# Filter norms and skip terms of a long convolution, from rows on every partition to channels on the partitions

## The chip, the cores and the metric

The kernel runs on one core of a Trainium2 chip. The core has a matrix engine (TensorE; PE in the profile, with its weight loads PEld), a vector engine (DVE), a scalar engine (ACT), GpSimd (POOL) and SyncE (SP), whose queue issues most DMAs. Each engine runs its own instructions in the order in which they were recorded and waits on semaphores for the others. The metric is the time of one execution on the device in microseconds (us), as the median of several runs.

## The reference

One layer of an encoder block over 2048 positions of width 1024, in float32. What matters here is the Hyena branch, 512 channels wide: two long convolutions, each with a filter of 4096 taps per channel that a small network generates. The filter is scaled to norm 1 per channel, and each convolution adds its input times a factor `d` per channel (the skip term):

```python
    h = h * decay[:, None, None, :]
    h_fwd = h[:, :, 0]
    h_bwd = h[:, :, 1]
    k = jnp.concatenate([h_fwd[:1] + h_bwd[:1], h_fwd[1:], jnp.zeros_like(h_fwd[:1]),
                         h_bwd[1:][::-1]], axis=0)
    return k * lax.rsqrt(jnp.sum(k * k, axis=0, keepdims=True) + EPS)
...
    uf = jnp.fft.rfft(uf32, n=2 * l, axis=1)
    y = jnp.fft.irfft(uf * k_freq[None], n=2 * l, axis=1)[:, :l]
    return (y + uf32 * d.astype(jnp.float32)).astype(u.dtype)
...
    z = v
    for n, gate in enumerate((x1, x2)):
        z = gate * fft_long_conv(z, k_freq[:, n], long_d[n])
    return z
```

Before this branch come the normed projection, and beside it a 2-D Fourier mix; after it the output projection and an MLP of width 4096.

## The kernel before

The stages follow each other: projection (to about 415 us), Fourier mix and filters side by side (to about 637), the two convolutions ("hyena"), output projection, and the two MLP products. All matrix products that must be exact to float32 are made of three products of a split operand: `split` writes a rounded part (`kh`) and a rest (`kl`).

The filters are computed in `filters`, in eight units: `Unit(ct, n)` is the block of 128 channels `ct` (0 to 3) of convolution `n` (0, 1); units 0 to 3 belong to n = 0, units 4 to 7 to n = 1. Positions lie on the partitions, channels along the free axis. A unit goes through four steps.

- `generate(q)`, q = 0 to 7: four matmuls into `pk`, times the decay on DVE (`kt`), the split into `kh` and `kl` (for units 1 and 4 both parts lie in one tile `k`), the square on ACT (`sqr`, one buffer), and its sum into `acc` on POOL. At q = 7 POOL folds acc to 128x128.
- `normalise`: from the sum over positions come the reciprocal root (the norm of the filter) and the skip term. Tap 0 sits on partition 0; its value `k0` becomes `k0 + d * v * rsqrt(v)`, where v is the sum of squares plus EPS, so that after the later scaling with rsqrt(v) the skip term d is left. The matmul with a matrix of ones gives the same sums on all 128 partitions, and DVE works on 128x128, then on one partition with 128 elements. It writes tap 0 of kh and kl, and a row of `norms`.
- `stage1(c)`, c = 0 to 7: three matmuls (`pk1`) on kh and kl and a transposition on DVE into `Gk`.
- `stage2(q)`, q = 0 to 7: four matmuls (`pk2`) on Gk, a copy on ACT (`ks`), and a DMA of the spectrum to DRAM.

The spectra are not scaled by the norms; `scale` multiplies the convolutions' first input `zz` by the product of both norms instead, half of it on POOL and half on DVE.

Units overlap: while unit i is in stage1 and stage2, unit i + 2 is generated, and unit i + 1 is normalised early in stage2 of unit i (`if i and new and q == 1`). The order that a reader of the code sees is not the order on each engine: the scheduler of the tile framework sets the instructions of an engine by priority and by when its own estimates say that they are ready, and the program keeps that order. A small matmul or a tiny DVE instruction can so come to stand ahead of work that the code names earlier. All PSUM tiles come from one ring of 8 banks (`pa`).

`rsqrt` is a helper: a square root on ACT (`sq_k`), a reciprocal on DVE (`rc_k`) and one Newton step (`nw_k`); tiles of one column take a shorter form with scalars from the tile.

Of the kernel before, what the change touches and what calls it, by code (L numbers as in the profile page):

```python
# [10 lines left out]
F32 = mybir.dt.float32  # L11
# [3 lines left out]
ALU = mybir.AluOpType  # L15

EPS = 1e-5
# [110 lines left out]
P = 128  # L128
# [6 lines left out]
def hybrid_block(ctx: ExitStack, tc: tile.TileContext, A, out):  # L135
    nc = tc.nc
# [24 lines left out]
    def pool(name, side="left"):  # L161
        return tc.tile_pool(name=name, bufs=1, side=side, reuse_waits="tile")

    def pa(nm):
        return ps.tile([P, 512], F32, tag="a", name=nm, bufs=8)

    def load(pl, tag, shape, src, bufs=1):
        t = pl.tile(shape, F32, tag=tag, name=tag, bufs=bufs)
        nc.sync.dma_start(t, src)
        return t  # L170

    ident = load(cpool, "ident", [P, P], A["ident"])
    gmix = load(cpool, "gmix", [P, 8], A["g_mix"])
    ones = cpool.tile([P, P], F32, tag="ones", name="ones")
    nc.vector.memset(ones, 1.0)

    def split(hi, lo, src, scale=None, eng=None):

        if scale is None:
            nc.scalar.copy(hi, src)  # L180
            (eng or nc.vector).tensor_sub(lo, src, hi)  # L181
        else:
            nc.scalar.mul(hi, src, scale)  # L183
            nc.vector.scalar_tensor_tensor(out=lo, in0=src, scalar=scale, in1=hi, op0=ALU.mult, op1=ALU.subtract)
# [7 lines left out]
    def rsqrt(v, pl, nm, keep=None):  # L192

        s, r = (pl.tile(list(v.shape), F32, tag=f"{a}_{nm}", name=f"{a}_{nm}") for a in ("sq", "rc"))
        q = pl.tile(list(v.shape), F32, tag=f"nw_{nm}{keep or ''}", name=f"nw_{nm}", bufs=keep)
        nc.scalar.sqrt(s, v)
        nc.vector.reciprocal(r, s)
        if v.shape[1] == 1:

            nc.vector.tensor_scalar(out=q, in0=r, scalar1=r, scalar2=v, op0=ALU.mult, op1=ALU.mult)  # L200
            nc.vector.tensor_scalar(out=q, in0=q, scalar1=-0.5, scalar2=1.5, op0=ALU.mult, op1=ALU.add)
            nc.vector.tensor_scalar(out=q, in0=q, scalar1=r, scalar2=None, op0=ALU.mult)
            return q
        nc.vector.tensor_mul(q, r, r)
        nc.vector.tensor_mul(q, q, v)
        nc.vector.tensor_scalar(out=q, in0=q, scalar1=-0.5, scalar2=1.5, op0=ALU.mult, op1=ALU.add)
        nc.vector.tensor_mul(q, r, q)
        return q
# [261 lines left out]
    def filters(ctx, fp, gp, zp, zzs, norms, emb, wo, e1k, f2):  # L470
# [2 lines left out]
        e1h, e1l = (fp.tile([P, P], FR, tag=n, name=n) for n in ("e1h", "e1l"))  # L473
        split(e1h, e1l, e1k)

        class Unit:
            def __init__(self, ct, n):
                self.ct, self.n = ct, n
# [34 lines left out]
                    nc.gpsimd.tensor_add(self.acc[:, 0, :], self.acc[:, 0, :], self.acc[:, 1, :])  # L513

            def normalise(self):
                p = pa("psum_k")
                nc.tensor.matmul(p[:, 0:128], lhsT=ones, rhs=self.acc[:, 0, :], start=True, stop=True)
                v = fp.tile([P, 128], F32, tag="vk", name="vk")
                nc.vector.tensor_scalar(out=v, in0=p[:, 0:128], scalar1=EPS, scalar2=None, op0=ALU.add)
                sc = rsqrt(v, fp, "k")  # L520
                nc.vector.tensor_copy(norms[:, self.n, self.ct], sc)

                dk = fp.tile([1, 128], F32, tag="dk", name="dk")
                nc.sync.dma_start(dk, A["long_d"][:, 2 * self.ct + self.n, :])
                nc.vector.tensor_mul(dk, dk, v[0:1, :])
                nc.vector.tensor_mul(dk, dk, sc[0:1, :])
                nc.vector.tensor_add(dk, dk, self.k0)
                hi, lo = (t[0:1, :, 0, :] for t in self.k)
                k0 = dk.rearrange("p (c j) -> p c j", c=8)
                nc.vector.tensor_copy(hi, k0)  # L530
                nc.vector.tensor_sub(lo, k0, hi)
                if self is units[7]:
                    nc.gpsimd.tensor_mul(norms[:, 0], norms[:, 0], norms[:, 1])

            def scale(self, q, eng):
                z = zzs[0][:, 4 * q : 4 * q + 4, 128 * self.ct : 128 * self.ct + 128]
                eng.tensor_mul(z, z, norms[:, 0, self.ct : self.ct + 1, :].broadcast_to([P, 4, 128]))

            def stage1(self, c):
                if c == 0 and self is units[7]:  # L540
# [18 lines left out]
        units = [Unit(ct, n) for n in range(2) for ct in range(4)]  # L559
# [11 lines left out]
        for i, u in enumerate(units):  # L571
# [12 lines left out]
            for q in range(8):  # L584
# [14 lines left out]
                j = 8 * i + q - 50  # L599
# [690 lines left out]
    with pool("ip") as ip, pool("cp1") as cp1:  # L1290
        with pool("cp0", "right") as cp0:
            run(project(ip, fx, (cp0, cp1), (1, 2), None), filter_hidden(cp0), fourier_weights(cp0))
        zstack, tabs, early = (ctx.enter_context(ExitStack()) for _ in range(3))
# [26 lines left out]

        run(project(ip, fx, (None, cp1), (-1, 0), uf), tables())
        e1f, e1k, turn, gy, e1z, wo, emb, f2 = got
    norms = early.enter_context(pool("norms", "right")).tile([P, 2, 4, 128], F32, tag="norms", name="norms")
    with pool("filters") as fp:
        zzs = []
        gp = early.enter_context(pool("gk", "right"))
        spx = early.enter_context(ExitStack())
        filt = filters(spx, fp, gp, zp, zzs, norms, emb, wo, e1k, f2)
        with pool("fourier", "right") as fo:
            ffs.insert(0, load(fo, "ff0", [P, 1, 2, P], A["ff"][:, 0:1]))  # L1330
            for i, _ in enumerate(fourier(fo, uf, e1f, ffs)):
                if i % 2 == 0 and i < 16 or 16 <= i < 24:
                    next(filt)
        run(filt)
# [84 lines left out]
```

## Time and profile before

| | |
|---|---|
| time, median of 3 runs | 2384.09 us (2382.59 to 2384.88) |
| the profiled execution | 2386.26 us, its span 2384.0 us |
| PE busy | 2257.1 us, 95% of the span |
| DVE / ACT / POOL busy | 1620.5 / 1105.3 / 1141.4 us |
| granted PE clock, mean | 0.981 of full speed |
| sums psum_k of units 0, 1, 2, 3 | at 446.8, 467.4, 499.6, 522.2 us |
| sums psum_k of units 4, 5, 6, 7 | at 545.0, 567.9, 589.3, 613.2 us |

The rows of the profile name line, engine, operation, what is written from what, and the shape. In a timeline row the first two numbers are start and length in us; what stands in brackets at the end is how long the engine had been idle and who ended it. A float32 matmul is shown as two passes ("x2").

### The profile page before, as it was taken

What the parts mean: (1) busy time and instruction counts of PE and PEld (TensorE: products, weight loads), DVE (VectorE), ACT (ScalarE), POOL (GpSimd) and SP (SyncE); (2) the same over time, 40 slices, a digit from 0 to 9 for tenths busy, and PEclk for the clock granted to TensorE, in tenths of its full rate; (3) what the DMA queues carried; (4) which work ended last, traced back from release to release, by engine and by line L of the source; (5) the groups of instructions that cost most, each with busy time, mean ns of one, the idle gap of its engine ahead of it and who ended that gap; (6) DMA issues with size and microseconds to landing.
All of it is one profiled execution on the core that took longest, in us unless ns stands there. A gap on an engine that the chain in (4) does not pass through costs nothing.

```text
span 2384.0 us, 30994 instructions
## 1 busy us (share of the span) xinstructions
PE 2257.1 (95%) x10984; PEld 1865.3 (78%) x10984; DVE 1620.5 (68%) x2392; ACT 1105.3 (46%) x1813; POOL 1141.4 (48%) x750
## 2 busy tenths in 40 slices
PE   8999999899899979997898999999989999899997
PEld 6887788788787858886677878888868888688886
DVE  6998444888777774456545334222289999999997
ACT  6553211565365554445444566555533333433334
POOL 4345323566565621227545555555345354635454
PEclk9999999999999999999999999999999999999999
DMA  7545621457698886567787454333394444754411
GB/s 255 173 146 175 215 80 58 153 186 228 215 207 192 204 225 181 173 195 245 244 259 247 157 191 145 111 118 107 134 345 159 166 156 145 252 172 144 149 53 71
DMA packets 287242, 418.85 MB, mean 176 GB/s; under 512 B 16677, under 2 KB 173679, under 8 KB 284785
## 3 DMA queue, kind: packets, MB, share of 16 engines
q1 hardware_dynamic: 284593, 412.45, 55.2%
q10 hardware_dynamic: 2496, 4.45, 0.6%
q8 instruction: 86, 1.41, 0.2%
q14 instruction: 67, 0.55, 0.1%
HBM read 288.16 MB, written 127.11 MB: 174 GB/s over the span
## 4 chain that ended last, share of the span: by engine, by line
PE 74%; DVE 10%; DMA 7%; ACT 3%; issue 3%; POOL 2%; SPq 1%; ACTq 0%; DVEq 0%; POOLq 0%
PE p2u L188 4%; PE p2u L190 4%; PE p2u L189 4%; PE p1u L188 4%; PE pu L189 4%; PE pu L190 4%; PE pu L188 4%; PE p1u L190 4%; PE p1u L189 4%; PE p2v L188 2%; PE p2v L189 2%; PE p2v L190 2%; PE po L190 2%; PE po L189 2%; PE po L188 2%
## 5 line engine op out<-in xcount | busy, mean ns | idle before, releaser
L188 PE MATMUL pu<-wh,xh 128*128 128x512 f32 x512 | 205.3, 402 | 5.4 <-ACT wh L183 5.4
L189 PE MATMUL pu<-wl,xh 128*128 128x512 f32 x512 | 202.0, 395 | 6.4 <-DVE wl L181 3.7
L190 PE MATMUL pu<-wh,xl 128*128 128x512 f32 x512 | 202.1, 395 | 0.0
L190 PE MATMUL p2u<-qbhm,qalm 128*128 128x512 f32 x504 | 196.1, 389 | 1.6 <-DVE qalm L181 1.6
L188 PE MATMUL p2u<-qbhm,qahm 128*128 128x512 f32 x504 | 196.1, 390 | 0.6 <-DVE acc L1199 0.6
L189 PE MATMUL p2u<-qblm,qahm 128*128 128x512 f32 x504 | 196.1, 389 | 0.0
L1199 DVE TENSOR_TENSOR acc<-acc,p2u 128x512 f32<-128x512 f32 x256 | 165.2, 678 | 9.4 <-PE p2u L190 8.8
L181 POOL TENSOR_TENSOR qblm<-rb,qbhm 128x1024 fp32r<-128x1024 f32 x48 | 146.4, 3054 | 38.2 <-ACT qbhm L180 38.2
L180 ACT CAST qahm<-s 128x1024 fp32r<-128x1024 f32 x64 | 67.3, 1054 | 204.9 <-PE p2u L189 96.4
L396 POOL TENSOR_TENSOR acc<-acc,cw 128x512 f32<-128x512 f32 x45 | 59.9, 1331 | 184.5 <-DVE acc L373 183.2
L181 POOL TENSOR_TENSOR alm<-W,ahm 128x512 fp32r<-128x512 f32 x63 | 88.0, 1398 | 124.6 <-ACT ahm L180 111.5
L957 DVE TENSOR_TENSOR c<-p1v,ku 128x512 f32<-128x512 f32 x64 | 44.1, 689 | 130.5 <-ACT ku L1003 100.8
L1163 POOL TENSOR_TENSOR s<-ra,s 128x1024 f32<-128x1024 f32 x16 | 39.2, 2449 | 193.3 <-DVE qalm L181 193.2
L181 DVE TENSOR_TENSOR qblm<-rb,qbhm 128x1024 fp32r<-128x1024 f32 x62 | 128.2, 2068 | 0.0
L188 PE MATMUL p1u<-bm,ahm 128*128 128x512 f32 x252 | 103.7, 411 | 22.9 <-ACT ku L1003 22.9
L180 ACT CAST qahm<-ra 128x1024 fp32r<-128x1024 f32 x46 | 48.5, 1054 | 165.8 <-PE p2v L189 103.9
L189 PEld LDWEIGHTS pu<-wl,xh 128*128 128x128 f32 x512 | 97.8, 191 | 28.6 <-DVE wl L181 4.1
L188 PEld LDWEIGHTS pu<-wh,xh 128*128 128x128 f32 x512 | 97.6, 191 | 27.2 <-ACT wh L183 7.0
L180 ACT CAST qbhm<-rb 128x1024 fp32r<-128x1024 f32 x110 | 115.1, 1047 | 5.5 <-DVE c L963 4.0
L188 PE MATMUL p2v<-qbhm,qahm 128*128 128x512 f32 x256 | 101.4, 396 | 16.7 <-DVE acc L1199 16.7
L180 ACT CAST ahm<-s 128x512 fp32r<-128x512 f32 x124 | 76.4, 618 | 82.4 <-POOL s L949 26.3
L190 PEld LDWEIGHTS pu<-wh,xl 128*128 128x128 f32 x512 | 97.5, 190 | 20.5
(387 smaller groups left out, 6859.7 us busy)
## 6 DMA issues: line engine op xcount, KB each, us to landing
W<-in_w_fc SPq DMA_DIRECT2D x66, 512.0 KB, 4.4
ks<-spec SPq DMA_DIRECT2D x128, 256.0 KB, 6.9
ra<-ad SPq DMA_DIRECT2D x32, 1024.0 KB, 5.3
rb<-td SPq DMA_DIRECT2D x64, 512.0 KB, 3.9
ad<-c SPq DMA_DIRECT2D x119, 256.0 KB, 3.2
rb<-in_w_fc SPq DMA_DIRECT2D x46, 512.0 KB, 3.8
dec<-in_decay SPq DMA_DIRECT2D x32, 512.0 KB, 4.5
spec<-ks SPq DMA_DIRECT2D x32, 512.0 KB, 2.8
```

The lines of the kernel that those rows point to most:

```text
L180: nc.scalar.copy(hi, src)
L181: (eng or nc.vector).tensor_sub(lo, src, hi)
L188: nc.tensor.matmul(o, lhsT=lh, rhs=rh, start=start, stop=False, skip_group_check=more)
L189: nc.tensor.matmul(o, lhsT=lh, rhs=rl, start=False, stop=False, skip_group_check=more)
L190: nc.tensor.matmul(o, lhsT=ll, rhs=rh, start=False, stop=stop, skip_group_check=more)
L396: nc.gpsimd.tensor_add(m1, m1, cw[:, 3, :])
L957: nc.vector.tensor_add(c, p, other)
L1163: G.tensor_sub(s2, a12, s2)
L1199: nc.vector.tensor_add(t, t, p)
```

## The change

`normalise` now takes `acc` as the stationary operand and a column of ones as the moving one, so that the sums come out as one column: channels on the partitions, 128x1. Root, reciprocal and Newton step run on 128x1, and one DVE instruction forms `dk = v * rsqrt(v) * d`. Two matmuls (`pdk`) bring dk back to one row and add k0 to it: dk against the identity, and k0 against a one. ACT rounds that row into tap 0 of kh, DVE writes the rest into kl, both from PSUM. The norms of a channel block are formed at its second unit (4 to 7): DVE multiplies both reciprocal roots (`both`), ACT spreads them over the identity (`diag`), and a matmul with ones (`pdiag`) writes the row to all partitions. The 8 loads of a row of long_d become two loads and one transposition at the start of the stage, and the product of all norms on POOL goes.

```diff
+        longd = fp.tile([P, 8], F32, tag="longd", name="longd")
+        rows = fp.tile([8, 128], F32, tag="dk8", name="dk8")
+        for n in range(2):
+            nc.sync.dma_start(rows[4 * n : 4 * n + 4, :], A["long_d"].rearrange("a (c n) j -> n (a c) j", n=2)[n])
+        p = pa("plongd")
+        nc.tensor.transpose(p[:, 0:8], rows, ident[0:8, 0:8])
+        nc.scalar.copy(longd, p[:, 0:8])
...
             def normalise(self):
+                i = units.index(self)
                 p = pa("psum_k")
-                nc.tensor.matmul(p[:, 0:128], lhsT=ones, rhs=self.acc[:, 0, :], start=True, stop=True)
-                v = fp.tile([P, 128], F32, tag="vk", name="vk")
-                nc.vector.tensor_scalar(out=v, in0=p[:, 0:128], scalar1=EPS, scalar2=None, op0=ALU.add)
-                sc = rsqrt(v, fp, "k")
-                nc.vector.tensor_copy(norms[:, self.n, self.ct], sc)
-                dk = fp.tile([1, 128], F32, tag="dk", name="dk")
-                nc.sync.dma_start(dk, A["long_d"][:, 2 * self.ct + self.n, :])
-                nc.vector.tensor_mul(dk, dk, v[0:1, :])
-                nc.vector.tensor_mul(dk, dk, sc[0:1, :])
-                nc.vector.tensor_add(dk, dk, self.k0)
+                nc.tensor.matmul(p[:, 0:1], lhsT=self.acc[:, 0, :], rhs=ones[:, 0:1], start=True, stop=True)
+                v = fp.tile([P, 1], F32, tag="vk", name="vk", bufs=2)
+                nc.vector.tensor_scalar(out=v, in0=p[:, 0:1], scalar1=EPS, scalar2=None, op0=ALU.add)
+                self.sc = rsqrt(v, fp, "k", 8)
+                dk = fp.tile([P, 1], F32, tag="dk", name="dk", bufs=2)
+                nc.vector.tensor_scalar(out=dk, in0=v, scalar1=self.sc, scalar2=longd[:, i : i + 1], op0=ALU.mult, op1=ALU.mult)
+                p = pa("pdk")[0:1, 0:128]
+                nc.tensor.matmul(p, lhsT=dk, rhs=ident, start=True, stop=False)
+                nc.tensor.matmul(p, lhsT=ones[0:1, 0:1], rhs=self.k0, start=False, stop=True)
                 hi, lo = (t[0:1, :, 0, :] for t in self.k)
-                k0 = dk.rearrange("p (c j) -> p c j", c=8)
-                nc.vector.tensor_copy(hi, k0)
+                k0 = p.rearrange("p (c j) -> p c j", c=8)
+                nc.scalar.copy(hi, k0)
                 nc.vector.tensor_sub(lo, k0, hi)
-                if self is units[7]:
-                    nc.gpsimd.tensor_mul(norms[:, 0], norms[:, 0], norms[:, 1])
+                if self.n:
+                    both = fp.tile([P, 1], F32, tag="both", name="both", bufs=2)
+                    nc.vector.tensor_scalar(out=both, in0=self.sc, scalar1=units[i - 4].sc, scalar2=None, op0=ALU.mult)
+                    diag = fp.tile([P, 128], F32, tag="diag", name="diag")
+                    nc.scalar.mul(diag, ident, both)
+                    p = pa("pdiag")
+                    nc.tensor.matmul(p[:, 0:128], lhsT=ones, rhs=diag, start=True, stop=True)
+                    nc.scalar.copy(norms[:, self.ct], p[:, 0:128])
...
-                eng.tensor_mul(z, z, norms[:, 0, self.ct : self.ct + 1, :].broadcast_to([P, 4, 128]))
+                eng.tensor_mul(z, z, norms[:, self.ct : self.ct + 1, :].broadcast_to([P, 4, 128]))
```

In the changed file lines behind line 474 stand 8 lower, those behind normalise 15 lower (pk at L503, pk2 at L567, kt at L507, zz at L552).

PE at unit 3, from the end of stage1 of unit 2 on; in these rows pk with a number is a tile of stage2 (from Gk). Before:

```order
L495 MATMUL pk<-wo,emb 128x128 x8
L552 MATMUL pk_4511<-Gk,f_2582 128x128 x4
L552 MATMUL pk_4518<-Gk,f_2582 128x128 x4
L517 MATMUL psum_k<-acc,ones 128x128
L495 MATMUL pk<-wo,emb 128x128 x4
L552 MATMUL pk_4560<-Gk,f_2582 128x128 x4
```

The same place on PE after:

```order
L503 MATMUL pk<-wo,emb 128x128 x8
L567 MATMUL pk_4512<-Gk,f_2582 128x128 x4
L567 MATMUL pk_4519<-Gk,f_2582 128x128 x4
L527 MATMUL psum_k<-ones,acc 128x1
L534 MATMUL pdk<-ident,dk 1x128
L535 MATMUL pdk<-k_4225,ones 1x128
L503 MATMUL pk<-wo,emb 128x128 x4
L567 MATMUL pk_4559<-Gk,f_2582 128x128 x4
```

The two pdk stand directly behind psum_k, ahead of the next unit's pk and of the rest of stage2; all eight units have it so, and in units 4 to 7 pdiag follows at once.

ACT at the same place, where sq_k is the root; before:

```order
L555 COPY ks<-pk_4511 128x512
L509 ACTIVATE sqr<-kt 128x512
L555 COPY ks<-pk_4518 128x512
L196 ACTIVATE sq_k<-vk 128x128
L180 CAST k<-kt 128x4x8x16
```

ACT after:

```order
L570 COPY ks<-pk_4512 128x512
L517 ACTIVATE sqr<-kt 128x512
L570 COPY ks<-pk_4519 128x512
L196 ACTIVATE sq_k<-vk 128x1
L538 CAST kh<-pdk 1x8x16
L180 CAST k<-kt 128x4x8x16
```

What stands ahead of the root is the same; the rounding of tap 0 comes to ACT behind it.

DVE at unit 5, with vk the sum plus EPS; before:

```order
L519 TENSOR_SCALAR vk<-psum_k 128x128
L525 TENSOR_TENSOR dk<-dk,vk 1x128
L499 TENSOR_TENSOR kt<-pk,dec 128x512
L197 RECIPROCAL rc_k<-sq_k 128x128
L181 TENSOR_TENSOR kl<-kt,kh 128x4x8x16
L204 TENSOR_TENSOR nw_k<-rc_k 128x128
L205 TENSOR_TENSOR nw_k<-nw_k,vk 128x128
L206 TENSOR_SCALAR nw_k<-nw_k 128x128
L499 TENSOR_TENSOR kt<-pk,dec 128x512
L207 TENSOR_TENSOR nw_k<-rc_k,nw_k 128x128
L521 COPY norms<-nw_k 128x128
L526 TENSOR_TENSOR dk<-dk,nw_k 1x128
```

DVE at unit 5 after:

```order
L529 TENSOR_SCALAR vk<-psum_k 128x1
L197 RECIPROCAL rc_k<-sq_k 128x1
L200 TENSOR_SCALAR nw_k<-rc_k,vk 128x1
L201 TENSOR_SCALAR nw_k<-nw_k 128x1
L202 TENSOR_SCALAR nw_k<-nw_k,rc_k 128x1
L532 TENSOR_SCALAR dk<-vk,nw_k,longd 128x1
L543 TENSOR_SCALAR both<-nw_k 128x1
L552 TENSOR_TENSOR zz<-zz,norms 128x4x128 x2
L539 TENSOR_TENSOR kl<-pdk,kh 1x8x16
L507 TENSOR_TENSOR kt<-pk,dec 128x512
```

The generation's kt and kl no longer stand between the steps of the norm but behind it, and the scaling of zz for the first channel block has moved here, between dk and kl; before, all of zz's scaling stood behind unit 7.

More of the change, by code (lines that the diff above doesn't have):

```diff
@@ L1322, in hybrid_block @@
         e1f, e1k, turn, gy, e1z, wo, emb, f2 = got
-    norms = early.enter_context(pool("norms", "right")).tile([P, 2, 4, 128], F32, tag="norms", name="norms")
+    norms = early.enter_context(pool("norms", "right")).tile([P, 4, 128], F32, tag="norms", name="norms")
     with pool("filters") as fp:
```

## The prediction

> **What bounds the kernel now.** I read the page first, then the busy time by stretches around the filter stage, then PE's waits there, then the timeline of one unit. The page (busy time; the chain that ended last):
>
> ```profile
> PE 2257.1 (95%) x10984; PEld 1865.3 (78%) x10984; DVE 1620.5 (68%) x2392; ACT 1105.3 (46%) x1813; POOL 1141.4 (48%) x750
> PE 74%; DVE 10%; DMA 7%; ACT 3%; issue 3%; POOL 2%; SPq 1%; ACTq 0%; DVEq 0%; POOLq 0%
> ```
>
> PE sets the end. The change touches only the filter stage, about 420 to 637 us. Its stretches, cut at the sums psum_k of units 1 to 7 and at the first matmul of the hyena stage (columns: stretch, length, busy PE, PEld, DVE, ACT, POOL, granted clock, DMA share, GB/s):
>
> ```profile
> 467.36:482.00 14.64, 11.98 (x69) 11.39 (x70) 12.94 (x23) 5.72 (x12) 6.89 (x5) 0.77 0.30 95
> 499.50:522.10 22.60, 20.90 (x157) 19.20 (x156) 20.68 (x34) 13.17 (x25) 15.56 (x13) 1.00 0.55 187
> 522.10:544.90 22.80, 20.77 (x156) 19.15 (x155) 20.99 (x34) 13.26 (x25) 15.61 (x14) 1.00 0.54 185
> 544.90:567.80 22.90, 20.92 (x157) 19.21 (x156) 21.09 (x34) 13.26 (x25) 15.71 (x14) 1.00 0.55 181
> 589.20:613.20 24.00, 19.72 (x132) 17.50 (x132) 17.43 (x29) 11.61 (x23) 15.67 (x13) 0.93 0.96 314
> 613.20:637.10 23.90, 20.25 (x139) 18.45 (x138) 17.79 (x28) 8.40 (x15) 14.09 (x9) 0.93 0.34 134
> ```
>
> One unit takes 22.6 to 22.9 us, PE works for 20.9 of it and DVE for 21: both are near their limit, and all that PE could win back is its idle 2 us per unit and the clock that is below 1.00. What PE waits for there (440 to 640 us; total, times, longest):
>
> ```profile
> PE pk L188 <- DVE kh L530: 6.9, 5, 2.7
> PE pk L552 <- DVE Gk L417: 6.5, 6, 2.7
> PE pk L189 <- DVE kl L531: 2.9, 4, 0.7
> PE psum_k L517 <- POOL acc L513: 2.2, 1, 2.2
> PE pk L189 <- DVE k L531: 0.7, 1, 0.7
> PE pk L188 <- DVE k L530: 0.7, 1, 0.7
> ```
>
> The chain of normalise (L530, L531) costs PE 11.2 us in all; the transposes, delayed by a busy DVE, 6.5.
>
> **The change part by part.** The long DVE instructions of normalise go and small ones on 128x1 come. The reciprocal shows the size:
>
> ```profile
> L197 DVE RECIPROCAL rc_k<-sq_k 128x128 f32<-128x128 f32 x8 | 7.6, 952 | 3.8 <-ACT sq_k L196 3.7
> ```
>
> 0.95 us before, 0.15 on 128x1 (a row below). Six more instructions over 128x128 shrink likewise, and five on one partition become one: DVE gets several us of air in each unit. That alone would be a gain, at most the waits above. But the changed order puts the new matmul pdk directly behind psum_k on PE, and pdk needs dk, the end of the whole chain. Before, PE had other matmuls to run while the chain went on. Unit 2 before:
>
> ```profile
> 499.39 0.63 ACT L509 ACTIVATE sqr<-kt 128x512 f32<-128x512 f32 x1 [0.84 <-POOL acc L510]
> 499.60 0.38 PE L517 MATMUL psum_k<-acc,ones 128*128 128x128 f32 x2
> 499.82 1.06 PE L495 MATMUL pk<-wo,emb 128*128 128x128 f32 x8
> 500.02 0.29 DVE L519 TENSOR_SCALAR vk<-psum_k 128x128 f32<-128x128 f32 x1
> 501.41 0.63 ACT L509 ACTIVATE sqr<-kt 128x512 f32<-128x512 f32 x1 [0.39 <-POOL acc L510]
> 501.94 0.57 ACT L555 COPY ks<-pk 128x512 f32<-128x512 f32 x1
> 502.41 0.31 ACT L196 ACTIVATE sq_k<-vk 128x128 f32<-128x128 f32 x1
> 509.28 0.47 PE L188 MATMUL pk<-kh,e1h 128*128 128x512 f32 x1 [0.35 <-DVE kh L530]
> ```
>
> PE went on at 499.82 and needed the result only at 509.28. The root started 2.4 us after psum_k ended (499.98): ACT has sqr and ks ahead of it, and sqr waits for POOL's accumulation. All of that hangs on matmuls ahead of psum_k, so it does not move when PE stops, and the order ahead of the root is unchanged. Unit 6, the last of the five such units, has 2.7 us; unit 7 has 0.4, since nothing waits for POOL there:
>
> ```profile
> 589.25 0.38 PE L517 MATMUL psum_k<-acc,ones 128*128 128x128 f32 x2
> 592.30 0.31 ACT L196 ACTIVATE sq_k<-vk 128x128 f32<-128x128 f32 x1
> 613.22 0.38 PE L517 MATMUL psum_k<-acc,ones 128*128 128x128 f32 x2
> 613.97 0.31 ACT L196 ACTIVATE sq_k<-vk 128x128 f32<-128x128 f32 x1
> 619.66 0.93 PE L188 MATMUL pk<-kh,e1h 128*128 128x512 f32 x3 [2.48 <-DVE kh L530]
> ```
>
> The rest of the chain, on 128x1, can be read at the kernel's end, where the same helper runs on such tiles:
>
> ```profile
> 2377.36 0.14 DVE L1239 TENSOR_SCALAR v_l<-ssq_l 128x1 f32<-128x1 f32 x1
> 2377.53 0.20 ACT L196 ACTIVATE sq_s<-v_l 128x1 f32<-128x1 f32 x1 [2.52 <-DVE v_l L1239]
> 2377.79 0.15 DVE L197 RECIPROCAL rc_s<-sq_s 128x1 f32<-128x1 f32 x1
> 2378.66 0.26 DVE L200 TENSOR_SCALAR nw_s<-rc_s,v_l 128x1 f32<-128x1 f32 x1
> 2378.96 0.15 DVE L201 TENSOR_SCALAR nw_s<-nw_s 128x1 f32<-128x1 f32 x1
> 2379.15 0.21 DVE L202 TENSOR_SCALAR nw_s<-nw_s,rc_s 128x1 f32<-128x1 f32 x1
> ```
>
> From the root's start: 0.20 + 0.06 to DVE + 0.15 + 0.26 + 0.15 + 0.21 + 0.26 for dk (taken like L200, it has two scalars too) and four gaps of 0.04 (2378.96 less the end at 2378.92) and 0.05 to PE: 1.5 us. With the DVE addition ahead (0.14 and a hop of 0.05) the floor of the chain is 1.75 us. So PE stands between 1.75 us (ACT and DVE free) and 2.7 + 1.5 = 4.2 us after psum_k. I take 4.0 for units 2 to 6, since POOL's accumulation, the cause of the 2.4 to 2.7, is not touched; and 0.4 + 1.5 = 1.9 for unit 7. PE does not step over a waiting matmul: at 467.36 psum_k of unit 1 waited 2.17 us for POOL and the pk matmuls, which need only tables, came behind it (below).
>
> A stop of this length also costs clock. Stretches right behind the waits of 2.7 and 2.48 us, and the sum of unit 1:
>
> ```profile
> 602.20:607.20 5.00, 4.27 (x11) 3.17 (x12) 4.13 (x6) 1.99 (x4) 1.43 (x2) 0.67 1.03 347
> 619.60:624.40 4.80, 4.74 (x18) 4.12 (x19) 4.54 (x8) 0.00 (x0) 4.80 (x3) 0.65 0.07 26
> 467.36 0.77 PE L517 MATMUL psum_k<-acc,ones 128*128 128x128 f32 x2 [2.17 <-POOL acc L513]
> ```
>
> 5.00 x 0.33 and 4.80 x 0.35 are 1.7 us lost each; in 467.36 to 482 two waits (2.2 and 2.7) lost 14.64 x 0.23 = 3.4. The waits of 0.7 lost nothing (1.00 in the steady units). So I charge 1.7 us for each stop of 4 us, and nothing for 1.9.
> The Trainium skill ("TensorE: Matmul & The Clock Gate", Part 1) says that the clock is halved after an idle window of about 3.4 us. By that a stop of 4.0 halves it, as I charge; but the trace shows the drop after 2.2 already, and the trace decides. If the stops came out at 3.3 (the transposes ahead of kt earlier, now that DVE has air), the page would give no drop and a sum of 20.5 - 5 x (0.7 + 1.7) = 8.5 us, the rows 20.5 - 3.5 = 17.
>
> The new matmuls: pdk is two fp32 products, four passes at 1.06 / 8 = 0.13, 0.55 us; pdiag two passes, 0.3 (units 4 to 7). psum_k gets narrower (0.1 won, not counted).
>
> Sum in us:
> - units 2 to 5: 4 x (4.0 + 0.55 + 1.7) + 2 x 0.3, less their share of the 11.2 (11.2 - 3.4 of unit 6 - 2.5 of unit 7 = 5.3): +20.3
> - unit 6: 4.0 + 0.85 + 1.7, less 2.7 + 0.7 and the 1.7 of clock that those cost: +1.5
> - unit 7: 1.9 + 0.85, less 2.5 and 1.7: -1.4
> - waits for the transposes of Gk apart from the 2.7 of unit 1: 3.8, of which 3.0 go with the lighter DVE: -3.0
> - units 0 and 1: unit 0 has a table load ahead of its root
>
> ```profile
> 446.84 0.39 PE L517 MATMUL psum_k<-acc,ones 128*128 128x128 f32 x2
> 450.22 1.28 ACT L196 ACT_TABLE_LOAD   x1
> ```
>
> so the stop lies between 1.75 + 1.28 = 3.0 and 451.5 - 447.2 + 1.5 = 5.8; I take 5.2 (ACT's work ahead is the same), + 0.55 + 1.7, less the 2.2 that PE waits for POOL anyway: 5.2. Unit 1: nothing ahead of its root, 1.75 + 0.55 + 1.7 clock, less the 2.7 behind a busy DVE and the 3.4 of clock: -2.1. Together +3.1.
>
> That is +20.5 us. Costed at nothing: the transposition of long_d (0.2 us on PE; its DMAs stand ahead of the dec loads, which issue at 406 and are used at 420); the waits of ACT (for hi) and DVE (for lo) for pdk and ACT's four small new instructions, since ACT is busy for 13 of 22.6 us and DVE has lost work, and PE stands at the same time; the eight dk loads that leave SP. The scaling of zz is cut up and moves forward to units 5 to 7; PE started on zz at 637.10, right behind its last filter product, so it wins nothing at the end.
> The profiled execution took 2386.26 (span 2384.0 and 2.3 around it), the median of the runs is 2384.09: the sum goes onto the median, 2404.6.
>
> **The rivals.**
> - *Stop without the clock loss* (17%): the clock falls only where PE is idle through a window of its own rhythm. Seven charges of 1.7 (units 0 to 6) go: 2392.7. Against it: four waits of 2.2 to 2.7 all show it.
> - *Short stop, faster* (6%): DVE and ACT come free early enough that the root starts at once; each stop is the floor. Then 4 x 2.3 + 0.6 - 5.3, 2.6 - 3.4 - 1.7, -1.4, -3.0, 3.0 + 0.55 - 2.2 and 2.3 - 2.7 - 3.4: -4.9 us, 2379. It decides from a stop below 1.75 + 4.9 / 6 = 2.6 us. Against it: sqr's wait for POOL in each unit. A stop near that point gives no change (5%).
> - *A new wait on DVE* (10%): in units 5 to 7 DVE's queue has zz's scaling between dk and kl, and it waits for the DMA of zz out of gates,
>
> ```profile
> DMA to landing us min/median/max: 8.5/8.5/8.5
> ```
>
> which lands 8.5 us after its issue. The issue waits for unit 4's last stage1 matmul, some 2 us ahead of psum_k of unit 5. That is 1 to 2 us after dk; with POOL's two scalings (1.6 us each) ahead of its accumulation, 4 us more: 2409.
>
> **How the numbers follow.** The forecast has 62%: 2404.6. Its own range, stops of 3.3 to 4.2 us (five units) and clock losses of 1.7 to 2.3, is 2401 to 2410. The low end 2391 takes in stops of 3.3 with no clock loss, nearly; the high end 2417 adds unit 0 without its 2.2 of cover, pdk at half clock (double, 3 us) and the wait for zz. Beyond it lie the faster and the unchanged case and a rest. Within 0.2% (4.8 us), about what a measurement of this kernel tells from no change, lie 5%; faster 6%; slower 89%.
>
> **What would show it.** In the profile after: PE waits for DVE dk in front of pdk, eight times, about 4 us in units 2 to 6, shorter in 1 and 7; the granted clock below 1.00 in the steady units; waits for kh and kl gone; DVE's busy time per unit several us below 21 and the units longer, 26 to 28 us. It is wrong if the root starts within a us of vk in those units, or if the clock stays at 1.00.

## The result, and the profile after

The changed kernel took 2410.62 us (median of 4 runs, 2408.43 to 2416.67) beside 2383.34 for the kernel before: a ratio of 1.0128, 95% interval 1.0093 to 1.0164. It is 27 us slower; 2404.6 was forecast, in a range of 2391 to 2417.

The profiled execution took 2412.35 us (span 2410.2). The page's busy times:

```profile
PE 2270.2 (94%) x11025; PEld 1876.8 (78%) x11025; DVE 1585.8 (66%) x2356; ACT 1110.9 (46%) x1830; POOL 1135.0 (47%) x749
```

DVE lost 35 us of work, and the time still rose. What PE waits for in the filter stage says why (total, times, longest):

```profile
PE pdk L534 <- DVE dk L532: 16.8, 4, 5.5
PE pdk L534 <- DVE both L543: 14.3, 4, 4.1
PE pk L567 <- DVE Gk L417: 1.6, 2, 0.8
```

All waits of before for `kh`, `kl` and `k` are gone; eight stops in front of pdk stand in their place. The row names `both` in units 4 to 7 because that is the last thing DVE did ahead; it is dk that pdk needs. Cut at the sums psum_k, the units read (columns as in the prediction; units 0, 1, 2, 5, 6, 7):

```profile
443.57:468.92 25.35, 19.83 (x142) 18.11 (x141) 14.30 (x33) 14.41 (x43) 12.59 (x11) 0.87 0.48 173
468.92:500.18 31.26, 28.32 (x205) 26.14 (x204) 21.41 (x38) 16.20 (x32) 17.87 (x15) 0.95 0.46 152
500.18:528.16 27.98, 23.82 (x160) 21.81 (x159) 15.48 (x29) 13.67 (x27) 15.10 (x13) 0.88 0.44 151
583.52:610.13 26.61, 22.47 (x154) 20.47 (x153) 17.76 (x32) 13.85 (x28) 20.00 (x16) 0.87 0.97 283
610.13:636.29 26.16, 21.33 (x138) 18.99 (x137) 16.82 (x27) 11.96 (x25) 18.21 (x15) 0.87 0.60 212
636.29:658.70 22.41, 19.59 (x146) 17.65 (x145) 9.66 (x18) 9.24 (x18) 3.47 (x2) 1.00 0.37 145
```

The sum over all eight units, in before and after (before up to 637.10, as in the prediction; its first matmul on zz came at 637.24, so that its stage is 190.4 us, and what follows from 190.3 shifts by 0.1):

```profile
sum 190.26, PE 169.87 PEld 156.15 DVE 160.11 ACT 102.28 POOL 122.08; mean PE 21.23 PEld 19.52 DVE 20.01 ACT 12.79 POOL 15.26
```

```profile
sum 215.13, PE 182.42 PEld 166.21 DVE 126.55 ACT 107.34 POOL 117.40; mean PE 22.80 PEld 20.78 DVE 15.82 ACT 13.42 POOL 14.68
```

A steady unit went from 22.6 to 28.0 us, while DVE's work in it fell from 20.7 to 15.5 and the clock from 1.00 to 0.88. The stop of unit 2, from the timelines of PE and ACT:

```profile
500.18 0.28 PE L527 MATMUL psum_k<-ones,acc 128*128 128x1 f32 x2
504.62 0.59 PE L534 MATMUL pdk<-ident,dk 128*1 128x128 f32 x2 [4.16 <-DVE dk L532]
505.65 2.07 PE L503 MATMUL pk<-wo,emb 128*128 128x128 f32 x8
```

```profile
500.01 0.63 ACT L517 ACTIVATE sqr<-kt 128x512 f32<-128x512 f32 x1 [0.85 <-POOL acc L518]
502.01 0.63 ACT L517 ACTIVATE sqr<-kt 128x512 f32<-128x512 f32 x1 [0.39 <-POOL acc L518]
503.02 0.20 ACT L196 ACTIVATE sq_k<-vk 128x1 f32<-128x1 f32 x1
```

The root starts at 503.02, 2.56 us after psum_k ended, behind the squares that wait for POOL. It is the place that the prediction named. In unit 1 the root has nothing ahead on ACT, but DVE comes to vk only at 470.37, 1.2 us after psum_k:

```profile
469.16 0.70 DVE L417 STREAM_TRANSPOSE Gk<-pk 128x512 f32<-128x512 f32 x1
469.80 0.64 DVE L181 TENSOR_TENSOR kl<-kt,kh 128x512 fp32r<-128x512 f32 x1
470.37 0.14 DVE L529 TENSOR_SCALAR vk<-psum_k 128x1 f32<-128x1 f32 x1
```

What the stop costs beside its length stands in the third row of unit 2: the eight pk passes behind it take 2.07 us; before, they took 1.06.

### The profile page after: what moved, and what is told of

Read it like the earlier page. It is cut to its first block, busy times and chain, and to the rows that moved or that the text cites. A ratio compares the mean times of both kernels' runs of the same rounds, so it can differ in the third digit from the quotient of the medians.

```text
span 2410.2 us, 31052 instructions
## 1 busy us (share of the span) xinstructions
PE 2270.2 (94%) x11025; PEld 1876.8 (78%) x11025; DVE 1585.8 (66%) x2356; ACT 1110.9 (46%) x1830; POOL 1135.0 (47%) x749
## 4 chain that ended last, share of the span: by engine, by line
PE 42%; DVE 5%; DMA 4%; issue 2%; ACT 1%; SPq 0%; POOL 0%; DVEq 0%; ACTq 0%; POOLq 0%
PE p2u L188 4%; PE p2u L190 4%; PE p2u L189 4%; PE p1u L188 4%; PE p1u L190 4%; PE p1u L189 4%; DMA w<-in_w_fc 2%; PE p2v L188 2%; PE p2v L189 2%; PE p2v L190 2%; PE p1v L188 2%; PE p1v L190 2%; PE p1v L189 2%; PE p2m L188 1%; PE p2m L189 1%
```

## The experiments

**The stop taken away.** e1_late splits normalise in two. `normalise` ends with dk; `finish` (pdk, tap 0, both, diag, pdiag) is called later:

```diff
+                self.dk = dk
+            def finish(self):
+                i = units.index(self)
                 p = pa("pdk")[0:1, 0:128]
...
                 if i and new and q == 1:
                     new.normalise()
                 generate(8 + q)
+                if new and q == (4 if i else 1):
+                    new.finish()
```

> The two pdk products, the writes of tap 0 and pdiag are recorded three to four steps of stage2 later, so that five groups of matmuls (about 1 us each) stand between psum_k and pdk. Theory (PE stops because pdk stands right behind psum_k, and the stop halves the clock): PE's waits for dk and for both fall from 31.1 us to under 3, the granted clock between the sums of units 0 and 7 rises from 0.88 to 0.97 or more, and the time falls below the kernel before: the waits for kh and kl (11.2) and most of those for Gk (4.9) stay away, 5.4 us of small matmuls stay: 2365 to 2376 us. Rival A (the small matmuls and the hops between engines cost it, wherever they stand): 2400 to 2412. Rival B (the clock falls in the filter stage for another reason than the stop): the waits go, the clock stays near 0.88, 2380 to 2390.

Measured: 2373.14 us, ratio to before 0.9976 (0.9959 to 0.9993). PE's waits in the stage, and units 2 and 6:

```profile
PE pk L571 <- DVE Gk L417: 5.0, 3, 3.0
PE pdiag L551 <- ACT diag L549: 2.1, 3, 1.1
PE pdk L538 <- DVE dk L532: 0.9, 4, 0.2
```

```profile
491.60:512.80 21.20, 20.99 (x161) 19.27 (x160) 15.36 (x29) 13.29 (x27) 15.10 (x13) 1.00 0.58 199
578.58:602.80 24.22, 20.13 (x138) 18.07 (x137) 15.47 (x27) 12.04 (x25) 18.64 (x15) 0.94 0.79 262
```

The same instructions in another place (in units 2 to 5 pdk now starts 4.8 us after the end of psum_k, and other matmuls fill 4.6 of it): 31.1 us of stops became 0.9, the clock is 1.00, a steady unit takes 21.2 us, and the stage (psum_k of unit 0 to pz) 177.3 against 215.1 of the changed kernel and 190.3 of before. Rivals A and B fall. The lighter norms are worth 13 us in the stage, once PE has other work beside the chain.

**The stop kept, PE kept busy.** e2_fill puts idle products between psum_k and pdk:

```diff
-                p = pa("pdk")[0:1, 0:128]
+                p = pa("pdk")
+                for _ in range(16 if i < 7 else 0):
+                    nc.tensor.matmul(p[:, 128:256], lhsT=ident, rhs=ident, start=True, stop=True)
+                p = p[0:1, 0:128]
```

> The changed kernel with 16 idle fp32 products of 128x128 (16 x 0.26 = 4.2 us at full clock) between psum_k and pdk in units 0 to 6; nothing else is moved. The chain is as long as before, but PE works through it. Theory (the stop is what halves the clock, about 3.1 us lost behind each stop of 4): the clock in the filter stage goes back to 0.98 or more; 6 x 3.1 + 1.7 are won, some 2 to 3 us lost since the filler is longer than the stops of units 1 and some others: 2390 to 2396 us. Rival (the clock follows the load of the stage, or the small matmuls themselves): the clock stays at 0.88 and the time at 2408 to 2416.

Measured: 2403.13 us, ratio 1.0102 (1.0072 to 1.0133). Units 2 and 6:

```profile
498.51:523.45 24.94, 24.55 (x193) 22.84 (x192) 15.47 (x29) 13.54 (x27) 15.11 (x13) 1.00 0.49 170
598.92:625.57 26.65, 22.66 (x171) 20.23 (x170) 17.17 (x29) 13.99 (x29) 19.52 (x15) 1.00 0.64 222
```

In units 1 to 6 only idle products stand between psum_k and pdk; in unit 0 the scheduler also put 1.7 us of useful products there. The clock is back at 1.00 although the kernel does more and its chain is as long: the lack of work on PE during the stop is what halves it. Units 2 to 4 won 2.5 to 3.0 us each. The size that I expected was too large: the total won 7.5, not 15 to 20. The stage won 11.6: unit 6 got nothing, since the chain took 6.2 us there (DVE waited 1.7 us for a DMA of the decay), and unit 7 lost 1.6, the cost of one half-clock window.

**The chain made shorter.** e5_root leaves pdk where it is, gives `sqr` two buffers and moves the root ahead:

```diff
-                    sq = fp.tile([P, 4, 128], F32, tag="sqr", name="sqr")
+                    sq = fp.tile([P, 4, 128], F32, tag="sqr", name="sqr", bufs=2)
...
-                nc.vector.tensor_scalar(out=v, in0=p[:, 0:1], scalar1=EPS, scalar2=None, op0=ALU.add)
-                self.sc = rsqrt(v, fp, "k", 8)
+                with tc.high_priority(offset=200):
+                    nc.vector.tensor_scalar(out=v, in0=p[:, 0:1], scalar1=EPS, scalar2=None, op0=ALU.add)
+                    self.sc = rsqrt(v, fp, "k", 8)
```

> The changed kernel with two buffers for sqr, so that ACT does not wait for POOL there, and with the sum's addition, the root and the reciprocal at a higher priority, so that the root stands ahead of two copies of ks on ACT. pdk stays right behind psum_k. Theory (the length of the stop is the lateness of the root; below some 2.2 us it costs no clock): stops of 2.0 to 2.4 us in units 1 to 7 and of about 3.5 in unit 0, clock 0.97 or more, time 2410.6 - 12.5 - 17 = 2378 to 2386 us. Rival A (the root is late for another reason, vk or acc): stops stay near 4, 2405 to 2412. Rival B (every stop costs the same clock, however short): stops of 2.0 to 2.4, clock about 0.88, 2396 to 2402.

Measured: 2395.44 us, ratio 1.0062 (1.0040 to 1.0084). PE's waits:

```profile
PE pdk L535 <- DVE dk L533: 10.8, 4, 4.4
PE pdk L535 <- DVE both L544: 9.2, 4, 3.6
```

Units 2 to 5 stop for 1.83 us, which is the floor of the chain; so the late root was the reason for 4 (rival A falls; which of the two edits brought it forward, no run takes apart). Units 0, 1 and 6 keep 4.4, 2.65 and 3.6. The time is some 9 us above the theory's 2378 to 2386. But units 3 and 5 lost clock with a stop of 1.83 and units 2 and 4 did not, which neither theory allows. The granted clock, read in steps of 0.2 us, shows why: it is half in pieces of 3.41 us or a multiple of that, on one fixed grid. Windows cut on that grid (the stop of unit 2 is 501.17 to 502.99, that of unit 3 is 523.89 to 525.71):

```profile
501.90:505.31 3.41, 2.32 (x19) 1.90 (x20) 1.63 (x6) 0.91 (x3) 2.87 (x3) 1.00 0.66 262
505.31:508.72 3.41, 3.41 (x33) 3.41 (x32) 1.57 (x3) 2.56 (x5) 1.29 (x1) 1.00 0.10 35
522.38:525.79 3.41, 1.58 (x16) 1.52 (x15) 2.78 (x8) 2.90 (x7) 3.33 (x3) 1.00 0.61 203
525.79:529.20 3.41, 3.41 (x15) 2.58 (x15) 0.67 (x2) 0.26 (x1) 1.71 (x2) 0.50 0.43 166
```

Unit 2's stop is cut by the edge at 501.90 and leaves 2.32 us of work in its window: no loss. Unit 3's lies in one window, which holds 1.58 us of work: the next window runs at half clock. The changed kernel on its own grid, around the stop of unit 2:

```profile
500.72:504.14 3.42, 0.00 (x0) 0.00 (x0) 0.78 (x4) 2.12 (x5) 3.42 (x3) 1.00 0.42 159
504.14:507.55 3.41, 2.93 (x13) 2.10 (x14) 0.58 (x3) 0.26 (x1) 0.28 (x1) 0.50 0.32 130
507.55:510.96 3.41, 3.41 (x18) 3.41 (x18) 1.38 (x2) 1.62 (x3) 1.25 (x1) 0.50 0.01 2
510.96:514.38 3.42, 3.42 (x32) 3.42 (x32) 0.69 (x1) 2.13 (x5) 0.87 (x2) 1.00 0.54 174
```

The empty window is followed by one at half clock; that one has 2.93 us busy at half speed, 1.47 us of full-speed work, and is followed by a second; 3.41 at half speed (1.71) is enough to get out. Six stops of 4 us or more cost two windows each in this way. Where a stop meets the grid counts as well: in after2, the changed kernel once more, the same six stops cost two windows each, but the stop of 2.94 us in unit 1, which cost one window here, costs none there, and the stop of 4.4 us in unit 0 of e5_root costs only one.

**The grid tested.** e6_fillroot is e5_root with the idle products of e2_fill, in numbers shorter than the stops, `(12, 6, 5, 5, 5, 5, 10, 0)[i]`.

> e5_root with idle fp32 products (0.12 us a pass, 2 passes each) between psum_k and pdk, somewhat fewer than the stop is long: 12 in unit 0, 6 in unit 1, 5 in units 2 to 5, 10 in unit 6. The chain and the moment at which pdk can run stay as they are; PE only does more. Theory (the clock is set on a fixed grid of 3.41 us: a window in which PE did less than about 1.4 to 1.6 us of full-speed work is followed by one at half clock; in e5_root five windows of 1.71 us lost each): no half-clock window in units 0 to 6, 5 x 1.7 less than e5_root between psum_k of unit 0 and pz: 197.2 - 8.5 = 188.7 us, total 2385 to 2389 us. Rival (the clock goes with the place or the small matmuls, not with PE's work in the window): half-clock windows behind the same units and 2393 to 2398.

Measured: 2381.31 us, ratio 1.0010 (0.9996 to 1.0023). The stage in e5_root, then in e6_fillroot:

```profile
445.63:642.86 197.23, 174.58 (x1255) 160.07 (x1254) 128.40 (x230) 105.69 (x223) 120.20 (x97) 0.96 0.58 194
```

```profile
445.36:631.80 186.44, 178.11 (x1350) 163.42 (x1349) 125.57 (x230) 105.69 (x223) 120.33 (x97) 1.00 0.61 205
```

Some 95 passes more, and 10.8 us less: not one half-clock window is left between psum_k of unit 0 and pz. But the idle products are not all that changed. The scheduler now also puts useful ones ahead of pdk in units 0 to 3 (1.5 us, 3.0 us, and 0.8 us twice); PE at unit 2:

```profile
494.70 0.28 PE L527 MATMUL psum_k<-ones,acc 128*128 128x1 f32 x2
494.84 1.36 PE L536 MATMUL pdk<-ident 128*128 128x128 f32 x10
496.03 0.83 PE L503 MATMUL pk<-wo,emb 128*128 128x128 f32 x6
496.80 0.38 PE L538 MATMUL pdk<-ident,dk 128*1 128x128 f32 x2
```

So part of the 10.8 us, of which 8.5 were expected, is theirs. In units 4 to 6 only idle products were added, and the half-clock windows of units 5 and 6 are gone there too: the loss hangs on PE's work in the window. Unit 6 is 1.7 us shorter for it; unit 5 only 0.2, since PE there waits 2.1 us for Gk instead of 1.0. With it the kernel is level with before, and still 8 us behind the one without stops.

**The scaling of zz.** The change lets zz be scaled as soon as a block's two norms stand, in units 5 and 6. e7_norms7 is e1_late with the scaling held until all stand:

```diff
-                    nc.scalar.copy(norms[:, self.ct], p[:, 0:128])
+                    nc.scalar.copy(norms[:, 1, self.ct], p[:, 0:128])
+                    if self is units[7]:
+                        nc.scalar.copy(norms[:, 0], norms[:, 1])
...
-                j = 8 * i + q - 50
+                j = 8 * i + q - 56
```

> e1_late, but the scaling of zz waits until the norms of all units stand, as in the kernel before (the rows of norms go to a second half of the tile and are copied when unit 7 is done). Theory A (the scaling, moved forward by the change, burdens DVE and POOL in units 5 and 6, where PE waits 1.2 and 3.0 us for Gk): these waits fall to under 1.5 together, units 5 and 6 take 43 to 44 us instead of 46.8, unit 7 stays under 22, the time is 2 to 4 us under e1_late. Theory B (units 5 and 6 are held by the DMA of zz and dec, not by the scaling): they stay at 46 or more, unit 7 gains 1 to 2 us of length, the time is equal to e1_late or up to 3 us above.

Measured: 2367.93 us, ratio 0.9943 (0.9923 to 0.9964). Units 5, 6, 7:

```profile
554.39:575.49 21.10, 20.39 (x154) 18.58 (x153) 14.21 (x28) 13.17 (x28) 13.44 (x12) 1.00 0.98 306
575.49:595.92 20.43, 18.78 (x138) 16.73 (x137) 13.94 (x25) 11.63 (x25) 14.29 (x13) 1.00 0.97 324
595.92:621.13 25.21, 21.25 (x146) 19.25 (x145) 15.70 (x24) 9.71 (x19) 12.27 (x8) 0.93 0.33 130
```

Half of each theory: units 5 and 6 take 41.5 us instead of 46.8 although the DMA share there is 0.97 to 0.98, so the scaling did burden them; unit 7 takes 25.2 instead of 20.7, because PE now waits 4.0 us there for transposes behind scalings on DVE. The stage is 0.4 us shorter.

e8_diag is e1_late with `both` and `diag` made right behind dk.

> e1_late with the product of both scales and the diagonal (DVE both, ACT diag) made right behind dk, ahead of the late part. Theory: pdiag's three waits for ACT (0.5, 0.5, 1.1) go, units 4 to 6 are 2 us shorter together, the time 1 to 2 us under e1_late, which a total cannot show and the stage can. Rival (ACT or DVE are late there whatever the order): the waits stay, or move to the copies behind them.

Measured: 2373.58 us, ratio 0.9979 (0.9966 to 0.9993). The rival holds: pdiag's waits stay.

```profile
PE pdiag L552 <- ACT diag L537: 1.6, 3, 0.6
```

They are 0.5, 0.5 and 0.6 us in units 4 to 6, for 0.5, 0.5 and 1.1 in e1_late; in unit 4 diag still stands behind the same two copies of ks on ACT, although it is recorded earlier. The three units together take 69.1 us for 68.8, and the stage takes 178.6: in unit 6 PE waits 3.3 us for Gk, and two half-clock windows follow instead of one.

To compare the best, e1_late and e7_norms7 ran again beside a third, e10_share (12 scalings on POOL, 4 on DVE).

> e1_late once more, beside e7_norms7 on one chip: their filter stages took 177.3 and 176.9 us, their medians 2373.1 and 2367.9 came from different rounds. Theory (the stage decides, the rest is scatter of the stages behind): within 0.15% of each other, both 0.2 to 0.5% under the kernel before. Rival (the later scaling wins behind the filter stage): e12 0.2% or more under e11.

> e7_norms7 once more, beside e11. Same theories: 2368 to 2374 with the filter stage at 177 and PE's wait of about 4 us for Gk in unit 7 by the first; under 2368 by the second.

> e7_norms7 with 12 of the 16 scalings of zz on POOL and 4 on DVE (8 and 8 before). Theory: PE's wait of 4.0 us for Gk in unit 7 comes from five scalings of 1.2 to 1.4 us ahead of transposes on DVE; with three, two shorter, it falls to 1.5 or less, its half-clock window of 1.7 goes, unit 7 takes 20 to 22 us instead of 25.2, the filter stage 172 to 174, the time 3 to 5 us under e12. Rival: POOL's twelve scalings (1.5 us each, to about 619) end last and pz of the convolutions waits for them: unit 7 at 24 or more, no gain.

Measured: 2373.71 us (ratio 0.9973, 0.9962 to 0.9984), 2370.15 (0.9961, 0.9950 to 0.9973) and 2369.45 (0.9960, 0.9946 to 0.9974), with stages of 177.8, 176.5 and 174.9 us. The order is e1_late, e7_norms7, e10_share. All three beat both kernels, by 0.3 to 0.4% and 1.5 to 1.7%. Among them the intervals overlap: e7_norms7 lies 3.6 us, 0.15%, under e1_late, at the edge of the theory and short of the rival's 0.2%, so the two are not told apart, though the kernel with the late scaling came out lower both times. e10_share's wait for Gk fell to 2.3, not to 1.5, its half-clock window stayed, and unit 7 took 23.5: a smaller gain than expected.

**What is not the stage.** after2, e4_before and before3 are the two kernels again, unaltered.

> The changed kernel once more, unaltered. Question: the convolutions (pz to the first pt_y) took 243.4 us in its first profile and 238.5 in that of the kernel before, 235.7 in a second one of before, 235.0 to 240.8 in three kernels of this study. Theory (scatter of that stage between executions): here it lies anywhere from 236 to 244. Rival (the change lengthens that stage): again 243 or more. In the filter stage half-clock windows follow each stop of 4 us again, in pairs; stops in all 30 to 32 us.

> The kernel before once more, for the stages outside the filters: in the profile of the changed kernel the projection was 3.3 us shorter and the convolutions 4.9 us longer, though their instructions did not change. Theory (scatter between executions: the convolutions keep the DMA queues at 0.9): here too projection and convolutions differ from the first profile by 1 to 5 us. Rival (the change itself moves them): both within 0.5 us of the first profile, 637.1 to 875.7 for the convolutions.

> The kernel before a third time, for the stages behind the filters. From pz to the end its two profiles took 1746.8 and 1742.2 us; the eleven profiles of the changed kernel and its variants took 1747.2 to 1751.5, though no instruction behind pz differs. Theory (the change lengthens what follows it by some 4 us, in a way not yet seen): 1742 to 1747 again. Rival (scatter, and two profiles are too few): 1748 or more.

Measured, the stage in after2, e4_before and before3:

```profile
444.90:658.09 213.19, 180.50 (x1254) 164.60 (x1253) 127.11 (x230) 107.43 (x223) 117.61 (x97) 0.90 0.53 179
```

```profile
447.66:635.97 188.31, 168.05 (x1215) 154.22 (x1214) 160.97 (x266) 101.83 (x209) 123.10 (x98) 0.97 0.60 203
```

```profile
444.36:630.47 186.11, 166.76 (x1214) 153.10 (x1213) 160.84 (x266) 101.92 (x209) 123.12 (x98) 0.98 0.61 206
```

The stage differs by 24.8 us in the first pair of profiles and by 24.9 and 27.1 here. The convolutions took 237.1 us in after2, so the 243.4 of the first profile was scatter. So is what stands ahead of the stage: psum_k of unit 0 came at 444.4 to 447.7 us in before and at 443.6 and 444.9 in the changed kernel. From pz to the end it is otherwise: 1741.2 to 1746.8 us in three profiles of before, 1747.2 to 1751.5 in all eleven of the changed kernel and its variants (means 1743.4 and 1749.0). The ranges do not overlap, if only by 0.4 us, and before3 fell on the side of its theory, a little under the expected 1742 to 1747: by these fourteen profiles the change costs some 5 us behind the filters, in instructions that are the same. That would also be why e1_late wins 13 us in its stage and only 6 to 7 in all. Most of it lies in the first MLP product, which takes 653.5 to 659.3 us in before and 658.7 to 663.2 in the eleven others. PE waits there for `ku`, 17.8 to 22.9 us in before and 22.2 to 26.7 in the others; both ranges overlap. Why is open: no run here takes that apart.

## Why the prediction was right, and where it was short

The forecast of slower, and its mechanism, stood: pdk right behind psum_k stops PE for the norm chain, the root is late behind sqr and POOL, and the stop costs clock. e1_late shows the first (the place decides), e5_root the second, e2_fill and e6_fillroot the third. The steady units take 26.6 to 28.0 us, as forecast (26 to 28); eight waits for dk, the kh and kl waits gone, DVE at 15.5: each sign of the last part is there.

By terms, for the stage from psum_k of unit 0 to pz (predicted, then measured; waits from PE's rows before and after):

| term | predicted | measured |
|---|---|---|
| stops | +28.9 | +31.1 |
| waits that go | -19.1 | -18.8 |
| small matmuls | +5.6 | about +4.4 |
| clock, net | +5.1 | about +8.1 |
| stage | +20.5 | +24.8 |

The first two are PE's idle time in the stage, 215.13 - 182.42 = 32.7 us after (31.1 and the 1.6 for Gk) and 190.26 - 169.87 = 20.4 before. The next two are its busy time, 12.5 us more for 10.7 predicted; I split them by e1_late, which has the same matmuls and a busy time of 169.3 with 1.7 lost in one half-clock window, against 169.9 with 6.7 lost in four of them before.

- Units 2 to 5: +20.3 was set for them ahead of the credit for Gk, +20.3 came out with it. The stops were 4.1 to 4.2 us for 4.0.
- The clock is the term that was mis-sized. I read 1.7 us per stop off the waits of before; that is one window of 3.41 us at half clock. A stop of 4 us costs two. Set against e1_late, unit 2 is 6.8 us longer: 4.0 of wait, and 2.8 of slow matmuls, pdk's own among them, for 1.7.
- Unit 0's stop was 5.5 for 5.2. Unit 1's was 2.9 for the floor of 1.75 (which I had charged 1.7 of clock, against my own "nothing for 1.9"; that one half-clock window did follow was luck, for in after2 none does): "nothing ahead of its root" was true of ACT and wrong of DVE, where a transpose and kl stood ahead of vk. Together +3.9 for +3.1.
- Unit 6: +2.2 for +1.5. Unit 7: a stop of 2.0 for 1.9, no clock loss, -1.5 for -1.4.
- Costed at nothing, and rightly: the transposition of long_d, the waits of ACT and DVE for pdk. The scaling of zz won nothing at the end, as said; that it burdens units 5 and 6 by some 5 us (e1_late against e7_norms7) I had not seen, and in the changed kernel PE's waits for Gk are only 1.6 us.
- The stage was 4.3 us too low, the total 6.0. The rest lies outside the stage and was in no term: in the two first profiles what stands behind pz took 4.7 us more and what stands ahead of the stage 3.3 less.

The rivals: "stop without the clock loss" (2392.7) is refuted by the half-clock windows behind seven of the eight stops. It was right that the clock has a rhythm of its own, but a window need not be idle to lose it (1.58 us of work in e5_root). "Short stop" (2379) needed stops under 2.6 us, and they were 4.0 to 4.2; e5_root has stops of 1.83 in four units and still takes 2395, since units 0, 1 and 6 stop for 2.65 to 4.4 us and two of the four short stops are followed by a half-clock window. "A new wait on DVE" for the DMA of zz came in unit 5, behind dk as foretold, but only for 1.0 us, and it cost PE nothing that the profile shows: PE's only waits in the stage are the stops and 1.6 us for Gk.

## What to carry to other kernels

A matmul that needs the end of a chain through two other engines must not be recorded right behind the matmul that starts the chain: leave as much other matmul work between them as the chain is long (here 4.2 us, five groups of 1 us), and a change that cost 1.3% wins 0.2 to 0.3%. Cost a stop of PE by its length and by the half-clock windows behind it (here 2.8 us on top of 4.2). Work taken off an engine that is not the bound is worth only the waits of the bound that it ends.

## What the runs showed of the hardware

The granted clock of PE is set on a fixed grid of 3.41 us. I cut nearly the whole span of the changed kernel's first profile on that grid (from 5 us to some 2355): counting a window's busy time of PE times its clock as its work, of 654 windows at full clock 22 were followed by one at half clock, and of these 21 held 1.28 us of PE's work or less and one 1.70; of the 632 followed by full clock all but one (0.68) held 1.66 or more. In e5_root the border is soft between 1.5 and 1.8. Work of 1.47 in a half-clock window kept the clock down, and 1.71 raised it again; elsewhere in the same trace 1.41 and 1.46 were enough, so this border is soft too.

The Trainium skill ("TensorE: Matmul & The Clock Gate", Part 1) gives a free-running window of 3413 ns, which this trace has, and lets the clock fall after an idle window. Here the window need not be idle: with 1.58 us of work in it the clock fell. So a wait of 1.83 us can cost 1.7 more or nothing, by where it meets the grid.
